# A hybrid recurrence and expert layer: the mixer in five token groups instead of four, and gathered rows paced closer

## The chip, the cores and the metric

One core of a Trainium2 chip runs the whole layer in one launch. The metric is the device time of one execution in microseconds; the runs before have a median of 3271.78 us. TensorE multiplies, VectorE and ScalarE and GpSimd work elementwise, SyncE issues the ordinary transfers and GpSimd the indirect ones (the gathers).

## What is computed

1024 tokens of width 1024 go through one layer and a last norm:

```
h   = rmsnorm(x);  proj = h @ w_in          # q, f, i, output gate, conv B C h, two merge gates
y_a = gated linear recurrence (8 heads x 64, chunks of 64 tokens, a 64x64 state per head)
y_b = B * causal_conv3(C * h)
x   = x + (sig(g_A) * (y_a @ w_hg) + sig(g_B) * (y_b @ w_conv)) @ w_out
h2  = rmsnorm(x)
# 8 heads: scores against two key sets of 128, top 16 of each, top 16 of the sums -> 128 experts
x   = x + sum over the picks of gate * gelu(u_e . h2) * v_e
out = rmsnorm(x)
```

The recurrence and the convolution carry a state from token to token, so groups of tokens run in order.

## The kernel before

**Two stages.** The mixer (all up to the picks) runs over groups of 256 tokens. The experts run in two ways: for tiles (128 tokens) 2 to 5 densely, over all 16384 experts, in a stage after the mixer (`dense`, line 1008); for tiles 0, 1, 6 and 7 by gathering the 128 picked rows of `peer_u` and then of `peer_v` (`gather`, line 890). One gathered row is an indirect transfer of 128x1024 f32 (0.524 MB) that GpSimd issues and one VectorE pass, line 930 for u, line 936 for v: 4 tiles x 128 x 2 = 1024 rows. Below, "row" means this.

**A group in the mixer.** `front` (line 486) transposes the normed tokens and does the convolution branch; `gates_b` and `gates_a` multiply the merge gates; `recurrence` runs four pairs of heads one behind the other (`decays`, then `chunks`); `post` (line 598) does w_hg, w_out (line 624), the second norm, the query matmuls and the key scores (line 657) with their top 16; `picks_of` makes the expert numbers of each tile (`idx`, line 864). The helper `whole` (line 245) holds nearly all weight matmuls: the weights of 128x128 stand, the group's tokens move, so a matmul has as many columns as the group has tokens. Each group fetches all weights again, in blocks that `block` (line 239) puts into a ring of six buffers of 4 KB per partition (`wraw`). In the trace an f32 matmul is two records.

**What sets the order.** `together` (line 381) runs these generators side by side: it always advances the one whose share of its expected TensorE time (T_REC, T_POST and so on) is least, so it sets the order of the work by a clock of its own. Rows come in through `paced` (line 367): as soon as tile 0 has its `idx`, a step of four rows (two u, two v, once both run), then a pause of ROW_STEP on that clock. In the mixer rows have four buffers of 4 KB (line 329), in the dense stage four more (line 363). In the dense stage `interleave` (line 410) spreads the steps that are left, of ROW_STEPS = 290, evenly over the stage's TensorE time. `all_gates` (line 955) makes the gate table of the dense tiles by one-hot products (line 997 on VectorE, line 974 on TensorE) beside the last two groups, from group FROM on. A scheduler then fixes each engine's order; each engine runs it in order.

Of the kernel before, what the change touches and what calls it, by code (L numbers as in the profile page):

```python
# [22 lines left out]
P = 128  # L23
D = 1024
KK = D // P
TOKENS = 1024
GROUP = 256
CHUNK = 64
HALF = CHUNK // 2
# [27 lines left out]
RUSH = 5.4  # L57
ROWS_AT_ONCE = 4
T_REC, T_GATES, T_W, T_POST, T_FRONT, T_PICK = 92.0, 6.4, 55.0, 92.0, 170.0, 10.89
T_SOON, T_ROWS, ROW_STEP = 300.0, 1e4, 7.5  # L60
FROM = 2
T_GB, T_FIRST = 27, 40.0
ROW_STEPS, T_DENSE = 290, 1330.0

# [59 lines left out]
class Layer:  # L124
# [198 lines left out]
    def schedule(self):  # L323

        nd, last = len(DENSE) * P, self.place_dense()
        self.wd = self.dram.tile([nd // TB, P, NKEYS, TB], F32, tag="wd", name="wd")
        self.wraw = self.ring(0, 4, 6)
        self.M = M = self.place()
        self.rows = self.ring(300, 4, 4)
        rows = self.gather(BY_ROW)  # L330
        with contextlib.ExitStack() as parts:
            for name in ("w", "h0", "h1", "yy", "y", "o"):
                parts.enter_context(self.fresh(name))
            parts.enter_context(self.fresh("a", side="right"))
            self.gmix, self.gffn = self.view(M.gmix_kb, [D]), self.view(M.gffn_kb, [D])
            self.nc.sync.dma_start(self.gmix, self.a["norm_mix_g"].broadcast_to([P, D]))
            G = [types.SimpleNamespace(no=g, n0=GROUP * g, q=g % 2, ready=False, conv=False) for g in range(TOKENS // GROUP)]
            run_all(self.front(G[0], self.first_norm(G[0])))
            self.nc.sync.dma_start(self.gffn, self.a["norm_ffn_g"].broadcast_to([P, D]))
            for g in G:  # L340
                must = [(self.recurrence(g), T_REC), (self.gates_b(g), T_GB), (self.gates_a(g), T_GATES)]
                more = []
                if g.no:
                    must.append((self.post(G[g.no - 1]), T_SOON if g.no == 1 else T_POST))
                    more.append((self.picks_of(G[g.no - 1]), T_PICK))
                if g.no + 1 < len(G):
                    nxt = G[g.no + 1]
                    more.append((self.front(nxt, list(self.first_norm(nxt))), T_FRONT if g.no else T_FIRST))
                if g.no == 1:
                    more.append((self.paced(rows), T_ROWS))  # L350
                if g.no == FROM:
                    M.lev = self.ring(48, 8)
                    more.append((self.all_gates(DENSE, G[3]), T_W))
                self.together(must, more)
            self.together([(self.post(G[3]), T_POST)], [], True)
        self.regions = ALWAYS | EXPERTS
        with contextlib.ExitStack() as parts:
            for name in ("v", "raw", "s1", "s0", "ht", "e0"):
                parts.enter_context(self.fresh(name))
            for name in ("e1", "ph"):  # L360
                parts.enter_context(self.fresh(name, side="right"))
            self.whi, self.wlo, self.wraw = last.whi, last.wlo, last.wraw
            self.rows.more(last.rows)
            self.interleave(zipped(self.dense(last, DENSE[0] * P, nd), self.picks_of(G[3]), 4), rows)
            run_all(rows)

    def paced(self, rows):
# [108 lines left out]
    def first_norm(self, G):  # L476

        nc, a, M = self.nc, self.a, self.M
        xs = [M.xs.take([D]) for _ in range(2)]
        for t, x in enumerate(xs):  # L480
            nc.sync.dma_start(x, a["x"][G.n0 + t * P:G.n0 + (t + 1) * P, :])
        for x, r in zip(xs, self.rstd(xs)):
            nc.vector.scalar_tensor_tensor(x, x, r, self.gmix, op0=ALU.mult, op1=ALU.mult)
            yield x

    def front(self, G, xs):

        nc, M, n = self.nc, self.M, GROUP
        G.ready = G.conv = False
        while G.no > 1 and self.posted < G.no - 2:  # L490
            yield 1
        G.h = h = self.view(M.h[G.q], [KK, n])
        G.y = y = self.view(M.y, [4, n])
        for t, x in enumerate(xs):
            self.transpose_whole(h, x, t)
            yield
        G.ready = True
        while self.mixed < G.no - 1:
            yield 1
        for j in range(4):  # L500
            cc = self.whole(self.w_in(BCC + j), h, KK, n)
            ccs = M.f0.take([n])
            nc.scalar.copy(ccs, cc[:, :n])
            ch = self.whole(self.w_in(BCH + j), h, KK, n)
            u = M.fu.take([n + 2])
            nc.vector.tensor_copy(u[:, 0:2], self.carry[:, j, :])
            nc.vector.tensor_tensor(u[:, 2:], ccs, ch[:, :n], op=ALU.mult)
            nc.vector.tensor_copy(self.carry[:, j, :], u[:, n:n + 2])
            yield
            cb = self.whole(self.w_in(BCB + j), h, KK, n)  # L510
            s = M.f1.take([n])
            nc.scalar.activation(s, u[:, 0:n], AF.Copy, scale=self.convw[:, j, 0:1])
            for i in (1, 2):
                nc.vector.scalar_tensor_tensor(s, u[:, i:i + n], self.convw[:, j, i:i + 1], s,
                                               op0=ALU.mult, op1=ALU.add)
            nc.vector.tensor_tensor(y[:, j, :], s, cb[:, :n], op=ALU.mult)
            yield
        G.conv = True
# [3 lines left out]

    def gates_b(self, G):

        nc, M, n = self.nc, self.M, GROUP
        while self.picked < G.no - 2 or not G.conv:
            yield 1
        G.mb = self.view(M.big[G.q], [KK, n])
# [8 lines left out]

    def gates_a(self, G):

        nc, n = self.nc, GROUP  # L540
        while self.picked < G.no - 2:
            yield 1
        G.sga = self.view(self.M.big[G.q] + 8, [KK, n])
        for c in range(8):
            gp = self.whole(self.w_in(BGA + c), G.h, KK, n)
            nc.scalar.activation(G.sga[:, c, :], gp[:, :n], AF.Sigmoid)
            yield

    def recurrence(self, G):

        nc, M, n, w = self.nc, self.M, GROUP, self.w_in
        while not G.ready:
            yield 1
        h = G.h
# [42 lines left out]

    def post(self, G):

        nc, a, M, n = self.nc, self.a, self.M, GROUP  # L600
        nt, n0 = n // P, G.n0
        mg = self.view(M.h[G.q], [KK, n])
        for c in range(8):
# [47 lines left out]
        def scores(c, qt):  # L651
# [6 lines left out]
            s = M.s.take([n])  # L658
            nc.scalar.copy(s, sp[:, :n])
            todo.extend((top[:, t, c, :], topi[:, t, c, :], s[:, t * P:(t + 1) * P]) for t in range(nt))  # L660
            if len(todo) == 8:
                self.top16(todo)
                todo.clear()

# [12 lines left out]
    def picks_of(self, G):  # L677

        while self.posted < G.no:
            yield 1  # L680
        for t in range(GROUP // P):
            yield from self.pick(G.n0 // P + t, G.top[:, t], G.topi[:, t], G.mem)
        self.picked = G.no

    def decays(self, qs, k, b):
# [1 line left out]

        nc, m = self.nc, GROUP  # L690
        lv = self.M.lev.take([8, m])
        for li, ln in enumerate(LEVELS):
            b0, b1 = halves(b, ln)
# [21 lines left out]

    def chunks(self, p, lv, el, qs, k, v, hgs, y):

        nc, M, m = self.nc, self.M, GROUP
        ops = [self.ps(), self.ps()]
        for t in range(m // P):  # L720
            gps = []
# [457 lines left out]
```

## Time and profile before

| | |
|---|---|
| device time, three runs | 3261.70, 3271.78, 3284.35 us (median 3271.78) |
| the profiled execution | 3261.81 us, span 3260.0 us |
| TensorE busy | 2805.7 us, 86% |
| VectorE busy | 2646.3 us, 81% |
| GpSimd busy | 1537.4 us, 47% |
| ScalarE busy | 1002.6 us, 31% |
| moved | 938 MB, 288 GB/s over the span |

The page gives busy times of engines as shares of the whole span; since the mixer and the dense stage have different limits, the rows below are cut by stage. "Idle before" and "waited for" name what ended an engine's wait.

### The profile page before, as it was taken

The numbers are of one execution on the slowest core, as the hardware profiler recorded it, in microseconds if no ns is written. First come the engines' busy times: TensorE is split into PE (matmuls) and PEld (weight loads), VectorE is DVE, ScalarE is ACT, GpSimd is POOL, SyncE is SP. The second block draws the span as 40 slices with busy tenths as digits, with TensorE's granted clock in tenths as the row PEclk, the third lists the DMA queues.
The fourth block names the chain that finished last, engine by engine and source line by source line (L and its number), as shares of the span: only waits on it lengthen the run. The fifth ranks groups of instructions, "written<-read, shape, count | busy, mean of one in ns | idle before, by whom it ended". The sixth has DMA issues, their size and how long they took to land.

```text
span 3260.0 us, 42632 instructions
## 1 busy us (share of the span) xinstructions
PE 2805.7 (86%) x14956; PEld 2380.9 (73%) x14956; DVE 2646.3 (81%) x5515; ACT 1002.6 (31%) x1537; POOL 1537.4 (47%) x1332
## 2 busy tenths in 40 slices
PE   8998999898986989944649999999999999999910
PEld 7887888687775878734537778888888888888800
DVE  2233378578899898998999999889989888898897
ACT  3223133413314553113333333333333333333200
POOL 0001025355554445565355665546555555465575
PEclk9998999798997989967859999999999999999955
DMA  6442548498884888978888899989999999999998
GB/s 200 142 127 91 171 137 278 159 350 280 289 320 130 325 326 307 318 253 305 280 287 306 287 369 362 351 306 359 367 338 343 343 349 344 308 370 347 331 356 297
DMA packets 321718, 937.98 MB, mean 288 GB/s; under 512 B 29280, under 2 KB 103520, under 8 KB 319456
## 3 DMA queue, kind: packets, MB, share of 16 engines
q0 software_dynamic: 147456, 536.94, 46.2%
q1 hardware_dynamic: 174048, 398.32, 35.0%
q8 instruction: 118, 1.93, 0.2%
q14 instruction: 96, 0.79, 0.1%
HBM read 889.01 MB, written 46.14 MB: 287 GB/s over the span
## 4 chain that ended last, share of the span: by engine, by line
PE 59%; DVE 23%; DMA 6%; issue 6%; POOL 3%; ACT 2%; SPq 0%; DVEq 0%; POOLq 0%; ACTq 0%
PE ps L1053 14%; PE ps L249 14%; PE ps L285 13%; PE ps L288 6%; DVE mem_g L936 5%; DVE mem_g L930 4%; DMA mem_g<-in_peer_u,idx 3%; DMA mem_g<-in_peer_v,idx 2%; PE ps L624 2%; PE ps L731 2%; PE ps L278 2%; PE ps L277 2%; PE ps L276 2%; DVE mem_y L997 1%; POOL mem_g L900 1%
## 5 line engine op out<-in xcount | busy, mean ns | idle before, releaser
L249 PE MATMUL ps<-mem_h,mem_w 128*128 128x256 f32 x3584 | 836.2, 391 | 2.9 <-DVE mem_z L534 2.9
L249 PEld LDWEIGHTS ps<-mem_h,mem_w 128*128 128x128 f32 x3584 | 692.9, 196 | 102.4 <-DVE mem_z L534 3.2
L900 POOL DMA_INDIRECT mem_g<-in_peer_u,idx x352 | 441.3, 1254 | 455.7 <-DVE mem_g L930 283.0
L900 POOL DMA_INDIRECT mem_g<-in_peer_v,idx x336 | 404.8, 1205 | 377.5 <-DVE mem_g L936 236.1
L1053 PE MATMUL ps<-mem_v,mem_ph 128*128 128x512 f32 x2304 | 552.2, 389 | 3.3 <-DVE mem_ph L237 2.6
L285 PE MATMUL ps<-mem_ht,mem_s 128*128 128x512 f32 x2048 | 508.5, 390 | 5.9 <-DVE mem_z L1064 5.9
L1053 PEld LDWEIGHTS ps<-mem_v,mem_ph 128*128 128x128 f32 x2304 | 432.0, 188 | 95.3 <-DVE mem_ph L237 4.9
L930 DVE SCALAR_TENSOR_TENSOR mem_g<-mem_g 128x1024 f32<-128x1024 f32 x352 | 444.9, 1270 | 41.6 <-DMA mem_g<-in_peer_u,idx 41.0
L936 DVE SCALAR_TENSOR_TENSOR mem_g<-mem_g 128x1024 f32<-128x1024 f32 x336 | 444.9, 1324 | 35.0 <-DMA mem_g<-in_peer_v,idx 33.8
L285 PEld LDWEIGHTS ps<-mem_ht,mem_s 128*128 128x128 f32 x2048 | 385.2, 188 | 87.8 <-DVE mem_z L1064 7.6
L236 ACT ACTIVATE mem_s<-mem_raw 128x512 fp32r<-128x512 f32 x256 | 161.3, 632 | 578.4 <-PE ps L285 550.6
L900 POOL DMA_INDIRECT mem_e<-in_peer_v,idx x176 | 224.9, 1278 | 195.2 <-DVE mem_g L936 153.7
L288 PE MATMUL ps<-mem_ht,mem_s 128*128 128x512 f32 x1024 | 273.7, 389 | 0.0
L900 POOL DMA_INDIRECT mem_e<-in_peer_u,idx x160 | 205.0, 1281 | 136.1 <-DVE mem_e L930 89.0
L696 POOL TENSOR_TENSOR mem_y<-mem_y 128x128 f32<-128x128 f32 x96 | 53.2, 554 | 413.7 <-DVE mem_y L565 413.6
L936 DVE SCALAR_TENSOR_TENSOR mem_g<-mem_e,mem_g 128x1024 f32<-128x1024 f32 x176 | 226.5, 1287 | 13.3 <-DMA mem_e<-in_peer_v,idx 7.7
L237 DVE TENSOR_TENSOR mem_s<-mem_raw,mem_s 128x512 fp32r<-128x512 f32 x256 | 180.0, 707 | 64.0 <-PE ps L288 50.3
L288 PEld LDWEIGHTS ps<-mem_ht,mem_s 128*128 128x128 f32 x1024 | 192.4, 188 | 40.0
L930 DVE SCALAR_TENSOR_TENSOR mem_e<-mem_e,mem_g 128x1024 f32<-128x1024 f32 x160 | 196.8, 1236 | 2.9 <-DMA mem_e<-in_peer_u,idx 2.9
L236 ACT ACTIVATE mem_v<-mem_z 128x1024 fp32r<-128x1024 f32 x128 | 129.5, 1053 | 185.5 <-PE ps L278 182.8
L857 POOL TENSOR_TENSOR mem_z<-mem_z 128x800 f32<-128x800 f16 x64 | 124.9, 1951 | 101.3 <-DVE mem_z L855 58.0
L978 ACT COPY mem_a<-ps 128x512 f32<-128x512 f32 x128 | 124.2, 1084 | 130.5 <-PE ps L974 79.5
(189 smaller groups left out, 3841.4 us busy)
## 6 DMA issues: line engine op xcount, KB each, us to landing
mem_w<-in_w_in SPq DMA_DIRECT2D x160, 512.0 KB, 4.8
mem_raw<-in_peer_ut SPq DMA_DIRECT2D x128, 512.0 KB, 7.1
mem_z<-in_peer_v SPq DMA_DIRECT2D x128, 512.0 KB, 6.7
mem_w<-in_w_query SPq DMA_DIRECT2D x64, 512.0 KB, 4.9
wd<-mem_a SPq DMA_DIRECT2D x16, 2048.0 KB, 9.9
mem_z<-wd SPq DMA_DIRECT2D x32, 1024.0 KB, 14.1
mem_w<-in_w_out SPq DMA_DIRECT2D x32, 512.0 KB, 7.9
mem_w<-in_w_conv SPq DMA_DIRECT2D x32, 256.0 KB, 3.4
```

What stands on the lines that cost most here:

```text
L236: self.nc.scalar.activation(hi, src, AF.Copy)
L237: self.nc.vector.tensor_tensor(lo, src, hi.bitcast(F32), op=ALU.subtract)
L249: self.nc.tensor.matmul(ps, w[:, kk, :], act[:, kk, :], start=kk == 0, stop=kk == k - 1)
L276: mm(ps, lh, rh, start=first, stop=False, **kw)
L285: mm(ps, w[kk][0], act[part][:, kk, :], start=kk == part == 0, stop=False)
L288: mm(ps, w[j][1], act[0][:, j, :], start=False, stop=j == k - 1)
L857: nc.gpsimd.tensor_tensor(pr, eq, ci[:, hd:hd + 1, :].broadcast_to([P, TOPK, NCAND]), op=ALU.mult)
L900: nc.gpsimd.indirect_dma_start(out=r, out_offset=None, in_=a[table], in_offset=bass.IndirectOffsetOnAxis(ap=self.idx[t][:, k:k + 1], axis=0))
L930: nc.vector.scalar_tensor_tensor(u, u, 1.0, h2, op0=ALU.mult, op1=ALU.mult, accum_out=wt[:, k:k + 1])
L936: nc.vector.scalar_tensor_tensor(acc, v, wt[:, k:k + 1], acc, op0=ALU.mult, op1=ALU.add)
L978: nc.scalar.copy(dst[:, :, 4 * h:4 * h + 4].rearrange("p a t -> p t a"), ps.rearrange("p (t a) -> p t a", t=4))
L1053: nc.tensor.matmul(acc[t][hf], pp[c][i][:, tk], vp[c][:, k, 512 * hf:512 * hf + 512], start=c == 0 and i == 0 and k == 0, stop=c == NKEYS ...
```

## The change

The groups become 128, 128, 256, 256 and 256 tokens. Group sizes, tile counts and expected times (`share`) follow from the group. ROW_STEP falls from 7.5 to 6.2. FROM goes from 2 to 3, which is the same tokens (512 to 767) as before, and the two big buffers alternate so that the last group has the one it had. The diff, cut to its core:

```
+GROUPS = (128, 128, 256, 256, 256)
-T_SOON, T_ROWS, ROW_STEP = 300.0, 1e4, 7.5
-FROM = 2
+T_SOON, T_ROWS, ROW_STEP = 300.0, 1e4, 6.2
+FROM = 3
...
-            G = [types.SimpleNamespace(no=g, n0=GROUP * g, q=g % 2, ready=False, conv=False) for g in range(TOKENS // GROUP)]
+            G = [types.SimpleNamespace(no=g, n=n, n0=sum(GROUPS[:g]), q=(len(GROUPS) + g) % 2, share=n / GROUP,
+                                       ready=False, conv=False) for g, n in enumerate(GROUPS)]
+            end = G[-1]
...
-                must = [(self.recurrence(g), T_REC), (self.gates_b(g), T_GB), (self.gates_a(g), T_GATES)]
+                must = [(self.recurrence(g), T_REC * g.share), (self.gates_b(g), T_GB * g.share),
+                        (self.gates_a(g), T_GATES * g.share)]
...
-                    must.append((self.post(G[g.no - 1]), T_SOON if g.no == 1 else T_POST))
-                    more.append((self.picks_of(G[g.no - 1]), T_PICK))
+                    old = G[g.no - 1]
+                    must.append((self.post(old), (T_SOON if g.no == 1 else T_POST) * old.share))
+                    more.append((self.picks_of(old), T_PICK * old.share))
...
-        xs = [M.xs.take([D]) for _ in range(2)]
+        xs = [M.xs.take([D]) for _ in range(G.n // P)]
...
-        nc, M, n = self.nc, self.M, GROUP
+        nc, M, n = self.nc, self.M, G.n
```

The last pair stands in `front`, `gates_b`, `gates_a`, `recurrence`, `post`, and alike in `decays`, `chunks` and `picks_of`.

Three places in the engines' order. TensorE, from the program's first matmul on; before (mem_h_153 is the transposed group, mem_w a weight block, mem_yy the convolution's result):

```order
L258 MATMUL ps<-c_ident,mem_a 128x128 x16
L249 MATMUL ps<-mem_h_153,mem_w 128x256 x112
L249 MATMUL ps<-mem_yy,mem_w 128x256 x4
L249 MATMUL ps<-mem_h_153,mem_w 128x256 x8
L258 MATMUL ps<-c_ident,mem_a 128x128 x8
```

and TensorE from the first matmul on in the changed kernel, whose lines are numbered a little higher:

```order
L259 MATMUL ps<-c_ident,mem_a 128x128 x8
L250 MATMUL ps<-mem_h_157,mem_w 128x128 x112
L250 MATMUL ps<-mem_yy,mem_w 128x128 x4
L250 MATMUL ps<-mem_h_157,mem_w 128x128 x8
L259 MATMUL ps<-c_ident,mem_a 128x128 x8
```

The sequence and the count of weight matmuls stay, each has half the columns, and half the transposes stand ahead.

VectorE where the first tile's expert numbers are made (`idx`), before; the first row (line 930) stands 29 lines of this list further on:

```order
L831 TENSOR_TENSOR mem_z<-mem_z 128x8x8
L767 SCALAR_TENSOR_TENSOR st_117<-st_118,el,ps 64x64 x2
L864 CAST idx<-mem_z 128x128
L818 CAST mem_z<-mem_z 128x256
L802 MAX mem_z<-mem_z 128x8 x8
L820 TENSOR_SCALAR mem_z<-mem_z 128x8x16
L804 MATCH_REPLACE rest<-mem_z 128x50
```

and VectorE at the first `idx` in the changed kernel (line 935 is the u row's pass, 512 to 521 the convolution of a following group):

```order
L863 TENSOR_REDUCE mem_z<-mem_z 128x16
L869 CAST idx<-mem_z 128x128
L521 TENSOR_TENSOR mem_yy<-mem_a,ps 128x256
L935 SCALAR_TENSOR_TENSOR mem_g<-mem_g 128x1024 x2
L512 TENSOR_TENSOR mem_a<-mem_a,ps 128x256
L935 SCALAR_TENSOR_TENSOR mem_g<-mem_g 128x1024
L513 COPY carry<-mem_a 128x2
L519 SCALAR_TENSOR_TENSOR mem_a<-mem_a,c_convw 128x256 x2
```

Rows follow at once, since the pick of a second tile of the same group no longer stands behind the first.

VectorE at the program's end, behind the dense tiles' last norm passes (line 951), before; these rows are the end of a longer run, 66 rows in all:

```order
L936 SCALAR_TENSOR_TENSOR mem_g<-mem_e_10537,mem_g 128x1024 x2
L936 SCALAR_TENSOR_TENSOR mem_g<-mem_e_10541,mem_g 128x1024 x2
L936 SCALAR_TENSOR_TENSOR mem_g<-mem_g 128x1024 x4
L936 SCALAR_TENSOR_TENSOR mem_g<-mem_e_10537,mem_g 128x1024 x2
L936 SCALAR_TENSOR_TENSOR mem_g<-mem_e_10541,mem_g 128x1024 x2
L936 SCALAR_TENSOR_TENSOR mem_g<-mem_g 128x1024 x4
```

and VectorE behind the same passes (line 956) in the changed kernel, the whole run up to the last tile's norm:

```order
L956 SCALAR_TENSOR_TENSOR mem_z<-mem_z,rstd,mem_raw 128x1024
L956 SCALAR_TENSOR_TENSOR mem_raw<-mem_raw,rstd 128x1024
L941 SCALAR_TENSOR_TENSOR mem_g<-mem_e_11853,mem_g 128x1024 x2
L941 SCALAR_TENSOR_TENSOR mem_g<-mem_e_11857,mem_g 128x1024 x2
L941 SCALAR_TENSOR_TENSOR mem_g<-mem_g 128x1024 x4
L941 SCALAR_TENSOR_TENSOR mem_g<-mem_e_11853,mem_g 128x1024 x2
```

66 rows behind the last dense norm became 10; the others stand earlier.

## Rows read from the trace of the kernel before

**Rows 1.** Windows by stage: bounds us, length, busy us by engine, clock, DMA share, GB/s.

```profile
0.00:452.00 452.00, 424.62 (x2519) 372.22 (x2519) 159.82 (x666) 138.18 (x237) 36.69 (x90) 0.97 0.46 145
452.00:681.50 229.50, 214.18 (x1243) 183.37 (x1242) 168.21 (x485) 68.64 (x111) 111.76 (x111) 0.90 0.65 221
681.50:1004.00 322.50, 274.05 (x1682) 236.19 (x1682) 273.96 (x834) 86.51 (x154) 166.81 (x156) 0.91 0.83 293
1004.00:1700.00 696.00, 494.84 (x3371) 435.26 (x3370) 632.72 (x1553) 254.68 (x370) 349.77 (x294) 0.83 0.81 286
1700.00:3107.00 1407.00, 1397.76 (x6146) 1153.87 (x6144) 1279.22 (x1796) 449.79 (x656) 775.59 (x595) 1.00 0.95 340
3107.00:3260.00 153.00, 0.21 (x1) 0.00 (x0) 132.36 (x186) 4.83 (x9) 96.75 (x89) 0.51 0.89 331
```

**Rows 2.** Timeline: start us, length, engine, line; VectorE at 492, TensorE at 680.

```profile
492.50 0.23 DVE L864 CAST idx<-mem_z 128x128 uint32<-128x128 f32 x1
...
679.80 1.89 PE L249 MATMUL ps<-mem_yy,mem_w 128*128 128x256 f32 x8
681.53 2.75 PE L624 MATMUL ps<-mem_w,mem_h 128*128 128x256 f32 x12
```

**Rows 3.** Groups by line and shape: VectorE's row passes, GpSimd's gather issues.

```profile
L930 DVE SCALAR_TENSOR_TENSOR mem_g<-mem_g 128x1024 f32<-128x1024 f32 x352 | 444.9, 1270 | 41.6 <-DMA mem_g<-in_peer_u,idx 41.0
L936 DVE SCALAR_TENSOR_TENSOR mem_g<-mem_g 128x1024 f32<-128x1024 f32 x336 | 444.9, 1324 | 35.0 <-DMA mem_g<-in_peer_v,idx 33.8
L936 DVE SCALAR_TENSOR_TENSOR mem_g<-mem_e,mem_g 128x1024 f32<-128x1024 f32 x176 | 226.5, 1287 | 13.3 <-DMA mem_e<-in_peer_v,idx 7.7 <-DMA mem_g<-x2d 4.3
L930 DVE SCALAR_TENSOR_TENSOR mem_e<-mem_e,mem_g 128x1024 f32<-128x1024 f32 x160 | 196.8, 1236 | 2.9 <-DMA mem_e<-in_peer_u,idx 2.9
...
L900 POOL DMA_INDIRECT mem_g<-in_peer_u,idx x352 | 441.3, 1254 | 455.7 <-DVE mem_g L930 283.0 <-issue 33.5 <-DVE mem_z L810 32.4
```

**Rows 4.** Windows of line 930, then of line 936, alone: VectorE in the tail.

```profile
3107.00:3260.00 153.00, 29.26 (x48) 0.51 0.89 331
...
3107.00:3260.00 153.00, 91.09 (x71) 0.51 0.89 331
```

**Rows 5.** Timeline, VectorE at the end: the last rows and the last norm pass.

```profile
3249.07 2.60 DVE L936 SCALAR_TENSOR_TENSOR mem_g<-mem_e,mem_g 128x1024 f32<-128x1024 f32 x2
...
3255.08 1.28 DVE L951 SCALAR_TENSOR_TENSOR mem_g<-mem_g,rstd,mem_e 128x1024 f32<-128x1024 f32 x1
```

**Rows 6.** TensorE's waits: us, times, longest; 490 to 1004, then 1004 to 1690.

```profile
PE ps L876 <- DVE mem_z L872: 27.6, 1, 27.6
...
PE ps L974 <- DVE mem_y L997: 74.2, 15, 16.6
```

**Rows 7.** Timeline of TensorE at 366 us; the group of line 657's weight loads.

```profile
366.31 0.61 PE L657 MATMUL ps<-mem_z 128*128 128x128 f32 x4
366.75 2.97 PE L249 MATMUL ps<-mem_h,mem_w 128*128 128x256 f32 x13
...
L657 PEld LDWEIGHTS ps<-mem_z 128*128 128x128 f32 x256 | 38.8, 196 | 17.6 <-ACT mem_z L669 6.8 <-issue 5.5 <-ACT mem_a L978 1.9
```

**Rows 8.** Windows of line 249 alone: TensorE, its weight loads, clock, DMA.

```profile
0.00:452.00 452.00, 311.16 (x1387) 263.72 (x1387) 0.97 0.46 145
```

**Rows 9.** Transfers: GB/s in 40 slices; issues, KB each, median us to landing.

```profile
GB/s 200 142 127 91 171 137 278 159 350 280 289 320 130 325 326 307 318 253 305 280 287 306 287 369 362 351 306 359 367 338 343 343 349 344 308 370 347 331 356 297
...
mem_w<-in_w_in SPq DMA_DIRECT2D x160, 512.0 KB, 4.8
...
mem_e<-in_peer_v,idx POOLq DMA_INDIRECT x176, 7.5
```

**Rows 10.** VectorE's waits from 490 to 1004 us: us, times, longest.

```profile
DVE mem_g L930 <- DMA mem_g<-in_peer_u,idx: 23.2, 17, 4.1
DVE mem_g L936 <- DMA mem_g<-in_peer_v,idx: 15.0, 13, 3.1
```

**Rows 11.** Transfers from 490 to 1004 us: the v rows' issues, median us to landing.

```profile
mem_g<-in_peer_v,idx POOLq DMA_INDIRECT x62, 7.0
```

More of the change, by code (lines that the diff above doesn't have):

```diff
@@ L340, in schedule @@
             for g in G:
-                must = [(self.recurrence(g), T_REC), (self.gates_b(g), T_GB), (self.gates_a(g), T_GATES)]
+                must = [(self.recurrence(g), T_REC * g.share), (self.gates_b(g), T_GB * g.share),
+                        (self.gates_a(g), T_GATES * g.share)]
                 more = []
                 if g.no:
-                    must.append((self.post(G[g.no - 1]), T_SOON if g.no == 1 else T_POST))
-                    more.append((self.picks_of(G[g.no - 1]), T_PICK))
+                    old = G[g.no - 1]
+                    must.append((self.post(old), (T_SOON if g.no == 1 else T_POST) * old.share))
+                    more.append((self.picks_of(old), T_PICK * old.share))
                 if g.no + 1 < len(G):
                     nxt = G[g.no + 1]
-                    more.append((self.front(nxt, list(self.first_norm(nxt))), T_FRONT if g.no else T_FIRST))
+                    more.append((self.front(nxt, list(self.first_norm(nxt))), (T_FRONT if g.no else T_FIRST) * nxt.share))
                 if g.no == 1:
@@ L352, in schedule @@
                     M.lev = self.ring(48, 8)
-                    more.append((self.all_gates(DENSE, G[3]), T_W))
+                    more.append((self.all_gates(DENSE, end), T_W))
                 self.together(must, more)
-            self.together([(self.post(G[3]), T_POST)], [], True)
+            self.together([(self.post(end), T_POST)], [], True)
         self.regions = ALWAYS | EXPERTS
@@ L363, in schedule @@
             self.rows.more(last.rows)
-            self.interleave(zipped(self.dense(last, DENSE[0] * P, nd), self.picks_of(G[3]), 4), rows)
+            self.interleave(zipped(self.dense(last, DENSE[0] * P, nd), self.picks_of(end), 4), rows)
             run_all(rows)
@@ L523, in gates_b @@
     def gates_b(self, G):
-        nc, M, n = self.nc, self.M, GROUP
+        nc, M, n = self.nc, self.M, G.n
         while self.picked < G.no - 2 or not G.conv:
@@ L538, in gates_a @@
     def gates_a(self, G):
-        nc, n = self.nc, GROUP
+        nc, n = self.nc, G.n
         while self.picked < G.no - 2:
@@ L549, in recurrence @@
     def recurrence(self, G):
-        nc, M, n, w = self.nc, self.M, GROUP, self.w_in
+        nc, M, n, w = self.nc, self.M, G.n, self.w_in
         while not G.ready:
@@ L598, in post @@
     def post(self, G):
-        nc, a, M, n = self.nc, self.a, self.M, GROUP
+        nc, a, M, n = self.nc, self.a, self.M, G.n
         nt, n0 = n // P, G.n0
@@ L660, in scores @@
             todo.extend((top[:, t, c, :], topi[:, t, c, :], s[:, t * P:(t + 1) * P]) for t in range(nt))
-            if len(todo) == 8:
+            if len(todo) == 4 * nt:
                 self.top16(todo)
@@ L680, in picks_of @@
             yield 1
-        for t in range(GROUP // P):
+        for t in range(G.n // P):
             yield from self.pick(G.n0 // P + t, G.top[:, t], G.topi[:, t], G.mem)
@@ L685, in decays @@
     def decays(self, qs, k, b):
-        nc, m = self.nc, GROUP
+        nc, m = self.nc, b.shape[-1]
         lv = self.M.lev.take([8, m])
@@ L716, in chunks @@
     def chunks(self, p, lv, el, qs, k, v, hgs, y):
-        nc, M, m = self.nc, self.M, GROUP
+        nc, M, m = self.nc, self.M, qs.shape[-1]
         ops = [self.ps(), self.ps()]
```

## The prediction

> **What bounds the kernel now.** I read the profile by stages first, then by what each stage waits for. The windows table [rows 1] cuts the span at five places. Up to 452 us the mixer runs on the first tokens alone: TensorE is busy 424.6 of 452 us, VectorE 159.8. From 452 to 681.5 us (where the second group's w_out matmuls begin [rows 2]) TensorE still has 214 of 229.5 us. From 681.5 to 1004 us both are loaded (274 and 274 of 322.5), and from 1004 to 1700 us VectorE is the full one (633 of 696 against 495). From 1700 us, where the dense stage starts, TensorE has 1397.8 of 1407 us: the dense stage is TensorE-bound and takes 6144 matmuls of 128x512 that follow each other at 0.227 us. After 3107 us TensorE is done, and for 153 us only gathered rows remain.
>
> The second thing to see is where these rows lie. A row is one VectorE pass over 128x1024 (lines 930 and 936), 1024 of them, 1.28 us each: 444.9 + 444.9 + 226.5 + 196.8 = 1313 us over 1024 [rows 3]. Counted by stage (line 930 leaves two records for each, line 936 one; the tail's rows are shown [rows 4], the other stages read alike): 44 by 681.5 us, 108 more by 1004, 194 more by 1700, 583 in the dense stage, 95 in the tail. The first could not start before the first tile's expert numbers were there, at 492.5 us [rows 2].
>
> So the tail is late row work. 153 us for 95 rows is 1.61 us each; at 0.524 MB a row and 331 GB/s [rows 1] the transfer alone is 1.58 us. Row work taken out of the tail is gained there one for one, and paid wherever it is put instead.
>
> **The change, part by part.** The row counts below are counted in the order of VectorE's instructions of both kernels; times come from rows of the trace.
>
> *Where the rows go.* Before the first dense Gelu product (line 1028) stand 348 rows in the old order and 473 in the new; between it and the last one 572 and 525; behind the last one 104 and 26. So 125 rows enter the mixer, 47 leave the dense stage and 78 leave the end.
>
> *Tail.* The last TensorE work stands where it stood. Behind it the new order has the sums of line 1112 (4 us), the small operations of two norms (about 8) and their two last passes (2.5), 12 rows at 1.58 us (19), two more norm passes (2.5), 10 rows (8 are fetched ahead, so by the VectorE price: 13), and then the same end as now: 3249.07 + 2.6 is the last row, 3260 the end [rows 5], 8.3 us. Together about 57 instead of 153: **-96 us**. Bounds -85 (all 22 rows at 1.58 and the norms in line) and -104 (rows all landed).
>
> *Dense stage.* TensorE's instructions are the same; VectorE has 47 rows fewer and was already not the bound (1279 of 1407). **0 us**, bounds -5 and +5.
>
> *Middle: from the w_out matmuls of tokens 256 to 511 to the dense stage.* TensorE's work is the same in both orders, instruction for instruction. VectorE's order has 316 rows here before and 343 after: 27 more, 34.6 us. In the part until all_gates starts (681.5 to 1004 us, VectorE 85% busy) there are 8 of them, which can lie under TensorE's work; the other 19 (24 us) fall where VectorE is 91% busy and TensorE waits for its one-hot products (74.2 us for line 997 [rows 6]). **+27 us**, bounds 0 and +45.
>
> *Head: to those same w_out matmuls, now 681.5 us.* Three sub-steps.
>
> First, the matmuls. 512 of the 2048 weight matmuls (line 249) belong to the first 256 tokens; they become 1024 with 128 columns. A matmul is two records. With 256 columns they start 0.216 us apart (8 in 1.73 us, from 679.80 to 681.53 [rows 2]); the trace has no weight matmul of 128 columns, but the key scores of line 657 are the same f32 shape with their own weight loads, and four of them start within 0.44 us (366.31 to 366.75), 0.11 each [rows 7]. So a half-size matmul costs 0.222 instead of 0.432 us, and the 1024 cost 227 us instead of 221: +6 us. The bound on the other side: a load lasts 196 ns [rows 7], and if it did not lie beside the matmul before it, nothing would be saved by halving the columns; that is a rival below. The Trainium skill's page "TensorE: Matmul & The Clock Gate" (Part 3, "The mechanism") says a weight load overlaps with matmuls in flight only where their row groups differ; these use all rows, so by it each half-size matmul would pay its loads openly. The records of line 657 don't bear that out: they start 0.11 us apart with their loads beside them. By the rule the sum would be some 215 us longer.
>
> Second, when rows may start. TensorE's 424.6 us up to 452 are 311.2 of line 249 [rows 8] and 113 of the rest; the first group of 128 tokens has as many line 249 records up to its last key scores (680 matmuls in either order) at half the price, 156 us, and half the rest, 57. With the 27 us of idle kept, that is 239 us; the pick chain to the expert numbers took 40 us (452 to 492.5) and works on one tile either way. So the first tile's numbers come at about 280 us, not 492.5.
>
> Third, what happens from 280 us to those w_out matmuls. TensorE's busy time in the head is 424.6 + 214.2 = 639 us now [rows 1] and 645 in the new kernel; 213 of it and some 37 in the pick chain's 40 us are done by 280, so 395 are left. VectorE's order has 130 rows ahead of that group's first product of line 606, against 32 now: 98 more, 126 us, on an engine that has 328 us of work in 681.5 [rows 1]. The stage where rows already run at 0.33 a us is 681.5 to 1004: without the one 27.6 us stall at line 876 [rows 6] TensorE is busy 274 of 295 us there, 93%. 395 at 93% is 425, so w_out comes at 705 us, +24 us. Transfers speak against so little. Weights are fetched once per group (160 blocks of w_in for four groups [rows 9]), and a fifth group fetches all of them again: 40 blocks of w_in, 16 of w_query, 8 of w_out and 4 of w_v at 512 KB, 16 of w_hg and w_conv at 256 KB and 1 MB of keys, 41 MB. Up to 681.5 us the old kernel moved 65.5 + 50.7 = 116 MB [rows 1]; the new one moves 41 MB of weights and 51 MB of rows more, 208 MB. By 280 us it has moved about 67: 680 matmuls at 65.5 KB, 56 of lines 588 and 624 at 131 KB, 6 MB of tokens, keys and prefetch, 9 MB in the pick chain's time. 141 MB in 425 us would be 332 GB/s. The mixer's slices reach 350 at most, and the stages with rows 286 to 293 on average [rows 1, 9]. At 310 GB/s, about halfway, it takes 455 us, with w_out at 735. I take that: **+53 us**, bounds +24 (TensorE alone) and +80 (293 GB/s: 481 us).
>
> Cover: a weight block of 512 KB lasts TensorE 3.46 us now and 1.78 us with 128 columns; six blocks are fetched ahead, so 10.7 us cover a landing of 4.8 us [rows 9]. When transfers are full and landings double, the cover is gone, and the loss is that of the 293 GB/s case. The extra 1.3 us table loads and issues of SP for a fifth group lie on engines that are far from full (ScalarE 138 of 452 [rows 1]).
>
> **Sum.** +53 + 27 + 0 - 96 = -16. The profiled execution took 3261.8 us by the clock outside (span 3260.0), the median of the three runs is 3271.8, 0.3% above it. 3261.8 - 16 = 3246, times 1.003 is 3256; I say **3255 us**.
>
> **The rivals.**
>
> *The mixer swallows the rows.* For it: VectorE idles 292 us before 452 us [rows 1], and rows made it wait for their transfer only 38 us in all from 490 to 1004 us [rows 10]. Against it: the 332 GB/s. Head +24, middle 0: -72, so 3190, or 3199 beside the median.
>
> *Transfers bound the head.* The first two groups' weights and the rows get no more than the stage mean of 293 GB/s: head +80, middle +27, net +11, 3283 beside the median. For it: the DMA share is 0.83 from 681.5 us on already. Against: slices at 350.
>
> *Rows come late, on the other side.* All rows in the mixer use four buffers. One turn of a buffer is the landing (7.0 us for the v rows [rows 11]), the issue on GpSimd (1.25 [rows 3]) and the multiply (1.28): four in 9.5 us, 0.42 rows a us; the middle needs 343 in about 1046, 0.33. VectorE runs in order, so a late row holds the recurrence's operations behind it, and TensorE behind those. At landings of 11.7 us the pace is 0.28 a us: 343 rows take 1221 us, +202; net +53 + 202 - 96 = +159, about 3431. It makes the kernel slower by 1% from head and middle together +129 on, which is a landing of 10.4 us. Against it: the rows that land in the busier second half take 7.5 us in the median, with twice the buffers [rows 9].
>
> *Weight loads bind.* For it: a load's 196 ns [rows 7] is more than 0.11, and if loads can't lie beside matmuls, the half-size ones cost 0.432 instead of 0.222: 1024 x 0.21 = +215 us, net +199, 3471. Against it: the starts of line 657. It is the case that the rule of the Trainium skill's page named above would give.
>
> **How the numbers follow.** Forecast 0.56 (its own range 3220 to 3280), swallowed 0.17, transfers 0.15, rows late 0.08, loads 0.04. A measurement of this kernel can tell about 1% from no change, that is below 3239 or above 3304. Below: the swallowed case and 0.20 of the forecast, 0.37. Above: the two slow cases and 0.03 of the transfer case, 0.15. Within: 0.48. The range reaches down to the swallowed case's edge and up past the transfer case, and leaves out the two slow ones: 3190 to 3310.
>
> **What would show it.** In the changed profile: the first idx at about 280 us (right if 260 to 310); 128-column records of line 249 about 0.11 us apart while nothing is waited for; the w_out matmuls of tokens 256 to 511 at about 735 us; the dense stage's first matmul at about 1780 us; 1407 us of dense stage; a tail of about 57 us. I am wrong if the first idx is not there by 350 us, if the slices between 280 and 735 us show TensorE waiting for weights, if row landings rise over 10 us, or if the dense stage gets longer than 1412 us.

## The result, and the profile after

The changed kernel takes 3245.16 us (median of 6 runs, 3238.13 to 3252.48) beside 3267.47 for the kernel before on the same chip: a ratio of 0.9927, 95% interval 0.9900 to 0.9955. That is 0.7% faster: less than the 1% that the prediction took for the least a measurement can tell, but clear of the noise, since the interval lies below 1. It is ten us below the 3255 that were forecast. The profiled execution took 3238.13 us (span 3236.4).

Windows by stage of the changed kernel, cut at the same events as [rows 1] (first `idx`, w_out of tokens 256 to 511, start of `all_gates`, dense stage, TensorE's end); columns as there:

```profile
0.00:301.00 301.00, 263.18 (x2271) 252.27 (x2272) 135.55 (x607) 126.57 (x240) 38.60 (x98) 0.94 0.71 240
301.00:743.40 442.40, 394.83 (x2523) 349.49 (x2522) 332.84 (x846) 149.34 (x255) 228.43 (x256) 0.92 0.85 305
743.40:1077.00 333.60, 275.16 (x1682) 238.72 (x1682) 291.69 (x848) 86.85 (x154) 172.28 (x170) 0.90 0.86 303
1077.00:1783.60 706.60, 498.25 (x3372) 436.31 (x3371) 654.97 (x1579) 259.18 (x373) 385.76 (x307) 0.83 0.82 292
1783.60:3190.30 1406.70, 1399.20 (x6145) 1157.19 (x6144) 1221.88 (x1713) 449.68 (x657) 736.10 (x549) 0.99 0.90 323
3190.30:3236.40 46.10, 0.19 (x1) 0.00 (x0) 40.18 (x85) 3.99 (x8) 15.95 (x14) 0.53 0.62 228
```

Against [rows 1]: the head is 62 us longer (743.4 for 681.5), the middle 22 (1040.2 for 1018.5), the dense stage the same, the tail 107 shorter (46.1 for 153); the sum is -24. TensorE's busy time in the head rose by 19 (263.18 + 394.83 against 638.80), so 43 of the 62 are idle time. The rise is in the weight matmuls, here in a window of the whole head, line 249 before and line 250 after (the first numbers are TensorE's busy time and its records):

```profile
0.00:681.50 681.50, 478.58 (x2096) 404.46 (x2096) 0.94 0.53 170
...
0.00:743.40 743.40, 499.44 (x3120) 458.35 (x3120) 0.93 0.79 278
```

The timeline answers to [rows 2, 7]: weight matmuls of 128 columns, the first expert numbers, and the w_out matmuls (line 629 now):

```profile
19.77 20.49 PE L250 MATMUL ps<-mem_h,mem_w 128*128 128x128 f32 x182
...
301.20 0.23 DVE L869 CAST idx<-mem_z 128x128 uint32<-128x128 f32 x1
...
743.45 1.89 PE L629 MATMUL ps<-mem_w,mem_h 128*128 128x256 f32 x8
```

182 half-size records in 20.49 us are 0.113 us each, with nothing waited for. The v rows of the tail, in a window of line 941 alone (its first numbers are the window's length and VectorE's busy time), answer to [rows 4]; 22 rows are left of 95:

```profile
3190.30:3236.40 46.10, 28.18 (x22) 0.53 0.62 228
```

What TensorE waited for longest in the head (us, times, longest), before, from 0 to 681.5 us:

```profile
PE ps L258 <- DVE mem_a L483: 15.9, 1, 15.9
PE ps L731 <- DVE mem_y L711: 11.2, 2, 7.1
PE ps L756 <- DVE st L767: 4.0, 6, 0.7
```

and in the changed kernel, from 0 to 743.4 us:

```profile
PE ps L761 <- DVE st L772: 21.7, 6, 12.7
PE ps L736 <- DVE mem_y L715: 17.1, 3, 8.6
PE ps L259 <- DVE mem_a L488: 14.5, 1, 14.5
PE ps L662 <- DMA mem_z<-in_keys: 11.4, 5, 3.8
PE ps L250 <- ACT mem_h L260: 7.4, 1, 7.4
```

Line 761 (756 before) is the recurrence's matmul with the state that line 772 makes; 736 (731) follows the decays of 715; 259 (258) are the program's first transposes. Line 662 waits for the transfer of a block of the key set, line 250 once for ScalarE's copy of the transposed tokens. No wait of a weight matmul is for a weight block.

A second profile of the same kernel shows how far such stages can be trusted. In it the head takes 754.1, the middle 1055.9, the dense stage 1405.9 and the tail 46.8. Its execution was the slowest of its 6 runs (span 3262.7; their median 3247.63), while that of the first profile was the fastest of its 6. Head and middle move by 11 and 16 us between them; dense stage and tail do not.

### The profile page after: what moved, and what is told of

Read it like the earlier page. It is cut to its first block, busy times and chain, and to the rows that moved or that the text cites. A ratio compares the mean times of both kernels' runs of the same rounds, so it can differ in the third digit from the quotient of the medians.

```text
span 3236.4 us, 45285 instructions
## 1 busy us (share of the span) xinstructions
PE 2830.8 (87%) x15988; PEld 2434.0 (75%) x15988; DVE 2677.1 (83%) x5673; ACT 1075.6 (33%) x1686; POOL 1577.1 (49%) x1392
## 4 chain that ended last, share of the span: by engine, by line
PE 56%; DVE 23%; DMA 9%; issue 5%; ACT 3%; POOL 3%; SPq 0%; DVEq 0%; POOLq 0%; ACTq 0%
PE ps L1058 15%; PE ps L286 14%; PE ps L250 10%; PE ps L289 7%; DVE mem_g L941 5%; DMA mem_g<-in_peer_u,idx 4%; DVE mem_g L935 4%; DMA mem_g<-in_peer_v,idx 4%; PE ps L277 2%; PE ps L278 2%; PE ps L279 2%; PE ps L736 1%; DMA mem_z<-in_keys 1%; DVE mem_z L863 1%; DVE mem_y L1002 1%
## 5 line engine op out<-in xcount | busy, mean ns | idle before, releaser
L250 PE MATMUL ps<-mem_h,mem_w 128*128 128x256 f32 (+1 forms) x4480 | 856.8, 350 | 10.4 <-ACT mem_h L260 8.7
L250 PEld LDWEIGHTS ps<-mem_h,mem_w 128*128 128x128 f32 x4480 | 743.4, 200 | 88.0 <-ACT mem_h L260 10.2
L905 POOL DMA_INDIRECT mem_g<-in_peer_u,idx x384 | 486.6, 1267 | 503.6 <-DVE mem_g L935 305.1
L905 POOL DMA_INDIRECT mem_g<-in_peer_v,idx x368 | 450.8, 1225 | 442.2 <-DVE mem_g L941 202.2
L941 DVE SCALAR_TENSOR_TENSOR mem_g<-mem_g 128x1024 f32<-128x1024 f32 x368 | 494.9, 1345 | 50.3 <-DMA mem_g<-in_peer_v,idx 50.0
L935 DVE SCALAR_TENSOR_TENSOR mem_g<-mem_g 128x1024 f32<-128x1024 f32 x384 | 487.1, 1272 | 38.4 <-DMA mem_g<-in_peer_u,idx 37.6
L905 POOL DMA_INDIRECT mem_e<-in_peer_u,idx x128 | 186.4, 1456 | 220.9 <-DVE mem_e L935 192.4
L905 POOL DMA_INDIRECT mem_e<-in_peer_v,idx x144 | 173.3, 1203 | 139.9 <-DVE mem_g L941 94.0
L941 DVE SCALAR_TENSOR_TENSOR mem_g<-mem_e,mem_g 128x1024 f32<-128x1024 f32 x144 | 184.3, 1280 | 1.3 <-DMA mem_g<-x2d 1.1
L701 POOL TENSOR_TENSOR mem_y<-mem_y 128x128 f32<-128x128 f32 (+1 forms) x120 | 60.1, 501 | 233.4 <-DVE mem_y L570 233.3
L935 DVE SCALAR_TENSOR_TENSOR mem_e<-mem_e,mem_g 128x1024 f32<-128x1024 f32 x128 | 156.7, 1230 | 1.5 <-DMA mem_e<-in_peer_u,idx 1.5
```

The source lines that it names most:

```text
L250: self.nc.tensor.matmul(ps, w[:, kk, :], act[:, kk, :], start=kk == 0, stop=kk == k - 1)
L905: nc.gpsimd.indirect_dma_start(out=r, out_offset=None, in_=a[table], in_offset=bass.IndirectOffsetOnAxis(ap=self.idx[t][:, k:k + 1], axis=0))
L935: nc.vector.scalar_tensor_tensor(u, u, 1.0, h2, op0=ALU.mult, op1=ALU.mult, accum_out=wt[:, k:k + 1])
L941: nc.vector.scalar_tensor_tensor(acc, v, wt[:, k:k + 1], acc, op0=ALU.mult, op1=ALU.add)
```

## The experiments

Lines of the changed kernel stand five above those of the kernel before: rows are lines 935 (u) and 941 (v), the transposes of a second norm 259, that norm's products 643, the pick's matmuls 881. "Head" is the time to the w_out matmuls of tokens 256 to 511, "middle" from there to the dense stage.

**The two halves alone.** First the groups without the shorter distance, then the distance without the groups.

```
-T_SOON, T_ROWS, ROW_STEP = 300.0, 1e4, 6.2
+T_SOON, T_ROWS, ROW_STEP = 300.0, 1e4, 7.5
```

> The new groups with the old ROW_STEP of 7.5. VectorE's order then has 440 rows ahead of the dense stage (473 in the changed kernel, 348 before), 567 in it (525, 572) and 17 behind its last Gelu product (26, 104). My theory (a row costs its 1.28 us of VectorE in the mixer, nothing in the dense stage, 1.6 us in the tail): 33 rows fewer in the mixer are worth 30 to 42 us, the dense stage stays at 1407 us, the tail at 35 to 45 us, so about 3195 to 3210 us beside 3245 for the changed kernel: the closer pace is then no part of the gain but a loss. Rival (the closer pace brings the gain, the groups cost): 3250 to 3270 us, no faster than the changed kernel.

3268.62 us, ratio 0.9987 (0.9972 to 1.0001): far above my theory's range, inside the rival's.

```
-T_SOON, T_ROWS, ROW_STEP = 300.0, 1e4, 7.5
+T_SOON, T_ROWS, ROW_STEP = 300.0, 1e4, 6.2
```

> The old four groups with ROW_STEP 6.2. The order has 390 rows ahead of the dense stage (348 before), 575 in it, 59 behind its last Gelu product (104). My theory: the tail loses 45 rows, -71 us; the mixer gets 42 more, between +27 (half of them hidden) and +54; together -44 to -17, about 3225 to 3250 us beside 3267 before. Rival (the mixer before 1000 us has room for rows only because the first numbers come earlier): the 42 rows cost more than their VectorE time, no gain, 3260 to 3280.

3276.14 us, ratio 1.0018 (1.0007 to 1.0030). Here too the time lies in the rival's range and not in my theory's. Neither half gains anything, though both shorten the tail (to 30 and 90 us from 153): their middles take 1073 and 1083 us, with 322 and 350 rows, and the changed kernel's with 343 rows takes 1040. So the middle does not go by the number of rows alone.

**Rows held back.** The changed kernel, its rows starting only when the second tile has its numbers:

```
-        while 0 not in self.idx:
+        while 1 not in self.idx:
```

> The changed kernel, with rows starting only when the second tile has its numbers: 16 rows stand ahead of the third group's first product of line 606 (130 in the changed kernel, 32 before), 348 ahead of the dense stage, 923 to its end, as before the change. So it is the price of the small groups alone. Theory 1 (the head's 62 us come from rows standing in VectorE's order between the recurrence's operations): w_out of tokens 256 to 511 at 690 to 705 us instead of 743, total 3275 to 3290. Theory 2 (the small groups themselves cost them, by short recurrences with nothing beside them): w_out at 725 to 743, total 3310 to 3330. Theory 3 (my prediction's, transfers): 157 MB by then at 310 GB/s after the first 67, w_out near 700, as theory 1; the next kernel tells these two apart.

3347.47 us, ratio 1.0231 (1.0214 to 1.0248). No theory's total holds, and the head lies between theory 1 and theory 2: it takes 714.2, the middle 1071 (TensorE stands 42.8 us at line 259 in it), the tail 150. Its windows of the head and of the tail:

```profile
0.00:301.00 301.00, 262.54 (x2260) 252.04 (x2261) 133.72 (x603) 126.03 (x240) 38.61 (x98) 0.94 0.71 238
301.00:714.20 413.20, 389.77 (x2535) 345.55 (x2534) 194.99 (x671) 143.84 (x250) 95.12 (x143) 0.95 0.56 185
...
3199.60:3349.50 149.90, 0.39 (x2) 0.00 (x0) 129.02 (x183) 4.97 (x11) 91.75 (x85) 0.52 0.88 328
```

So of the head's 62 us the small groups cost 33 with hardly any rows (24 in the head, 44 before the change; TensorE 13.5 busier, 19 more idle), at 185 GB/s, far from full transfers; the 115 rows more of the changed kernel cost 29, a quarter us each.

**A quarter of the weights.** The changed kernel, where the second group of 128 tokens fetches a quarter of each weight block; the rest of its weights is left out, the matmuls stay. The edit, cut to its core (`thin` is set while the second group's work is handed in):

```
+        part = dims[0] // 4 if self.thin else dims[0]
-        self.nc.sync.dma_start(raw, src)
+        self.nc.sync.dma_start(raw[:, :part], src[:, :part])
...
```

> The changed kernel, where the second group of 128 tokens fetches only a quarter of each weight block and uses what lies in the rest of the buffer: about 30 MB less in the head, TensorE, VectorE and rows as they are (140 rows instead of 130 ahead of the third group's line 606). It leaves out part of that group's weights. My prediction's theory (transfers bound the head): the 30 MB at 310 GB/s are worth most of 97 us of transfer time, so w_out of tokens 256 to 511 comes at 705 to 715 us instead of 743, total 3210 to 3220. Rival (waits for VectorE and ScalarE, and the half clock behind them): w_out stays within 8 us of 743, total 3238 to 3252.

3245.23 us, the time of the changed kernel. Its head:

```profile
0.00:301.00 301.00, 262.14 (x2283) 251.99 (x2284) 138.87 (x609) 126.39 (x240) 39.74 (x99) 0.95 0.59 194
301.00:759.40 458.40, 396.94 (x2510) 350.90 (x2510) 343.44 (x855) 152.54 (x257) 249.25 (x264) 0.90 0.78 270
```

With 270 instead of 305 GB/s the w_out matmuls come no sooner: 759.4, beside 743.4 and 754.1 in the changed kernel's two profiles (this execution, at 3252.19 us, was the slowest of its four). The 30 us that the transfers' theory asked for are not there. Transfers don't bound the head.

**What holds the middle of the halves.** TensorE's waits with the groups alone, 1160 to 1572 us:

```profile
PE ps L259 <- DVE mem_z L643: 55.0, 1, 55.0
PE ps L881 <- DVE mem_z L877: 32.2, 1, 32.2
```

ScalarE in that wait (start, length, line; in brackets idle time before it and what ended it). Line 947 is the Gelu of a block of gathered products, 230 the square of a norm, first tile 0's last norm (mem_g), then the group's second norm (mem_z):

```profile
1250.21 1.28 ACT L947 ACT_TABLE_LOAD   x1
1295.91 0.23 ACT L947 ACTIVATE mem_g<-mem_g 128x32 f32<-128x32 f32 x1 [44.42 <-DVE mem_g L935]
1299.21 1.06 ACT L230 ACTIVATE junk<-mem_g 128x1024 f32<-128x1024 f32 x1 [3.07 <-DVE mem_g L941]
...
1300.39 1.06 ACT L230 ACTIVATE junk<-mem_z 128x1024 f32<-128x1024 f32 x1
```

And VectorE, one row after the other, most of them waiting for their transfer:

```profile
1287.67 1.22 DVE L935 SCALAR_TENSOR_TENSOR mem_g<-mem_g 128x1024 f32<-128x1024 f32 x1 [1.29 <-DMA mem_g<-in_peer_u,idx]
...
1289.71 1.29 DVE L941 SCALAR_TENSOR_TENSOR mem_g<-mem_g 128x1024 f32<-128x1024 f32 x1 [0.81 <-DMA mem_g<-in_peer_v,idx]
1291.85 1.23 DVE L935 SCALAR_TENSOR_TENSOR mem_g<-mem_g 128x1024 f32<-128x1024 f32 x1 [0.85 <-DMA mem_g<-in_peer_u,idx]
```

The group's norm stands behind tile 0's last norm, and this behind the 288th row (tile 0's last v row). In the code both norms, and the sixteen largest of the pick, take one scratch buffer (`rest`, one copy), and the norms share four small vectors. Where tile 0's norm was handed in first, the others must wait for its rows; in VectorE's order 22 rows stand together just ahead of it. New theory A: this shared scratch, not the rows' number, spoils the halves. In the changed kernel row 288 is done in time; ScalarE there squares tile 0's norm 44 us ahead of the group's, and TensorE's wait at line 259 is 2.7 us:

```profile
1198.71 1.06 ACT L230 ACTIVATE junk<-mem_g 128x1024 f32<-128x1024 f32 x1 [0.58 <-DVE mem_g L941]
...
1242.77 1.06 ACT L230 ACTIVATE junk<-mem_z 128x1024 f32<-128x1024 f32 x1
```

The test gives tile 0's norm scratch of its own (a row buffer for the square, and likewise its own `ms`, `rstd`, `rs_y`, `rs_t`), in the groups alone; the edit, cut to its core:

```
-        r, = self.rstd([x])
+        r, = self.rstd([x], self.rows.take([D]), "_own")
...
-        junk = self.small.tile([P, D], F32, tag="rest", name="junk", bufs=1)
+        if junk is None:
+            junk = self.small.tile([P, D], F32, tag="rest", name="junk", bufs=1)
...
```

> The small groups with the old distance of 7.5 between row steps, as in the run with the groups alone (3268.6 us, where TensorE stood 55 us before the transposes of a norm, line 259), but the last norm of a gathered tile takes scratch of its own (the square's output in a row buffer, its four small vectors under names of their own) in place of the scratch that all norms share. In VectorE's order the 22 rows that stood together ahead of that norm are spread, and 431 rows instead of 440 stand ahead of the dense stage. Theory A (the shared scratch chains the norm of the third group behind the norm of tile 0, and so behind the 288th row; TensorE waits for that): the 55 us wait falls under 20, the stage from the w_out matmuls of tokens 256 to 511 to the dense stage falls from 1073 to about 1030, total 3220 to 3235. Theory B (the rows' count and their VectorE time make the middle long): 9 rows fewer, 12 us, total 3250 to 3262.

3227.34 us, ratio 0.9874 (0.9851 to 0.9897), 18 below the changed kernel. The middle takes 1015 us instead of 1073. Its windows with the groups alone, then with own scratch (length first, the third busy time is VectorE's):

```profile
752.40:1825.40 1073.00, 785.54 (x5054) 683.22 (x5052) 919.77 (x2397) 346.48 (x527) 518.02 (x461) 0.83 0.79 278
...
752.40:1767.50 1015.10, 774.52 (x5053) 673.66 (x5051) 905.41 (x2378) 340.87 (x524) 507.73 (x447) 0.85 0.81 287
```

VectorE is 14 us less busy (9 rows fewer) and 44 less idle.

ScalarE now squares the group's norm first, and tile 0's 85 us later:

```profile
1230.55 1.06 ACT L231 ACTIVATE junk<-mem_z 128x1024 f32<-128x1024 f32 x1
...
1234.71 1.05 ACT L231 ACTIVATE junk<-mem_z 128x1024 f32<-128x1024 f32 x1
...
1319.76 1.06 ACT L231 ACTIVATE mem_g<-mem_g 128x1024 f32<-128x1024 f32 x1 [4.35 <-DVE mem_g L942]
```

and the transposes (line 260 here) wait 1.6 us:

```profile
1250.11 1.97 PE L260 MATMUL ps<-c_ident,mem_z 128*128 128x128 f32 x8 [1.60 <-DVE mem_z L644]
```

**The same in the other half.** The distance alone, with that scratch:

> The kernel before with the distance of 6.2 between row steps, as in the run with the step alone (3276.1 us, where TensorE stood 84.6 us for the pick's product of line 872), and scratch of its own for the last norm of a gathered tile. 360 rows instead of 390 stand ahead of the dense stage, and 85 instead of 59 behind the last first-half product of that stage. Theory A (in the run with the step alone the pick's sixteen largest waited with the shared scratch for tile 0's norm and its 288th row): the longest wait of TensorE ahead of the dense stage falls from 84.6 to 50 or less, the stage from the w_out matmuls of tokens 256 to 511 to the dense stage falls from 1078 to 1025 to 1045, the tail grows from 90 to about 130, total 3255 to 3275. Theory B (the wait is the pick chain's own length plus its rows): the longest wait stays over 70, the stage falls by the 30 rows' 38 us at most, total 3275 to 3290.

3252.57 us, ratio 0.9955 (0.9943 to 0.9967). TensorE's wait for the pick, 1092 to 1700 us, with the distance alone (us, times, longest):

```profile
PE ps L876 <- DVE mem_z L872: 131.7, 2, 84.6
```

and with own scratch:

```profile
PE ps L877 <- DVE mem_z L873: 78.9, 2, 43.5
```

The middle falls from 1083 to 1011, more than theory A asked; the 30 rows that left it are part of that, 38 us at 1.28 each. The tail is 131, as expected, and the total a little below the range.

**Own scratch where nothing is late for it.** First in the kernel before, then in the changed kernel.

> The kernel before with scratch of its own for the last norm of a gathered tile and nothing else; 347 rows instead of 348 ahead of the dense stage, 104 behind its last first-half product in both. In VectorE's order the norm of the last group stood behind tile 0's norm, which waits for the 288th row, with three rows between the products it needs and that row. Theory A: those three or four rows, 5 to 10 us, are saved in the middle; total 3255 to 3268, so nearly the same as the kernel before: the shared scratch was no large cost until rows came earlier and closer. Theory E (own scratch helps by itself, and the good of the run with the small groups came from it and not from the earlier rows): 3225 or less.

3273.88 us, ratio 1.0024 (1.0013 to 1.0036): no gain, a little beyond the expected range.

> The changed kernel with the same scratch of its own for the last norm of a tile. Its order of VectorE hardly changes (474 rows instead of 473 ahead of the dense stage, no rows in a clump in either), because the 288th row was already done when the third group's norm came. Theory A (the shared scratch matters only where rows are late for it): same as the changed kernel, 3240 to 3250. Theory C (own scratch helps by itself, by more slack at every norm): 3225 or less.

3260.05 us, ratio 0.9960 (0.9943 to 0.9977): not the 3240 to 3250 expected. By the ratios it is some 10 us slower than the changed kernel (0.9927 and, below, 0.9933), but the intervals overlap. Head 750.2, middle 1051.6, dense stage 1410; the stages are those of the changed kernel's second profile. Whether own scratch costs anything here is open. Both runs say that it is no gain by itself.

**Rows that stand together, but not ahead of the norm.**

```
-T_SOON, T_ROWS, ROW_STEP = 300.0, 1e4, 6.2
+T_SOON, T_ROWS, ROW_STEP = 300.0, 1e4, 5.9
```

> The changed kernel with a distance of 5.9 between row steps in place of 6.2. 474 rows instead of 473 stand ahead of the dense stage, but 12 of them now stand together, up to the 288th, ahead of tile 0's last norm, and the products that the third group's norm needs (line 635) come behind that norm. Theory A (only the shared scratch makes rows cost TensorE there, and this norm is free of it in time): no wait over 25 us for line 259, total 3238 to 3255. Theory D (rows that stand together cost wherever they stand, some 2 us each, for they run at the pace of the transfers): about 25 us more, total 3262 to 3275.

3254.58 us, ratio 0.9956 (0.9939 to 0.9972), inside theory A's range, at its upper edge; the wait at line 259 is 2.7 us, as A says. The middle of 1054.6 is that of the other runs with as many rows.

**Faster handing out in the dense stage.**

```
-ROW_STEPS, T_DENSE = 290, 1330.0
+ROW_STEPS, T_DENSE = 290, 1290.0
```

> The changed kernel with the assumed TensorE time of the dense stage 1290 in place of 1330, which hands the rows out faster in that stage: 1008 rows stand ahead of the last first-half product of that stage instead of 998, and the last norms of two more tiles follow without rows between them. Theory (the tail is priced by its late rows, 1.6 us each, and the dense stage has VectorE time to spare): dense stage unchanged at 1407 us, tail 46 to about 34, total 3230 to 3238. Rival (VectorE near the end of the dense stage is already as full as it can be, so that rows put there hold TensorE): dense stage 1412 or more, total 3243 to 3255.

3239.01 us, ratio 0.9902 (0.9881 to 0.9923): tail 35.5 and dense stage 1406.0, about as expected. It is 6 below the changed kernel, which the intervals don't separate.

**The best and the changed kernel side by side.**

> The changed kernel once more, beside the next one on the same chip, to see how far two profiles of one kernel differ by stage. Total 3240 to 3250; the w_out matmuls of tokens 256 to 511 and the dense stage's first matmul within 10 us of the first profile's 743.4 and 1783.6. Were the first profile's stages a rare case, they would move by 20 or more.

> Small groups, the old distance of 7.5 and scratch of its own for a tile's last norm, once more. If it beats the changed kernel: 3220 to 3235, 10 to 25 us below the run beside it, and no wait of TensorE for line 260 over 20 us behind 1100 us. If the first result was chance: within 5 us of the run beside it.

3247.63 (ratio 0.9933, 0.9917 to 0.9950) and 3231.06 (0.9885, 0.9865 to 0.9904): the groups with the old distance and own scratch beat both kernels, the changed one by 17 us. That the changed kernel's second profile would lie within 10 us of its first was wrong (754.1 for 743.4, and the dense stage at 1810.0 for 1783.6): by the expectation's own sign, a move of 20 or more, the first profile's stages are not typical. Windows of the own-scratch kernel's middle, dense stage and tail:

```profile
753.90:1773.70 1019.80, 769.19 (x5054) 670.64 (x5052) 907.99 (x2381) 340.83 (x524) 506.70 (x448) 0.86 0.81 286
1773.70:3189.80 1416.10, 1400.59 (x6144) 1155.79 (x6144) 1281.40 (x1779) 449.86 (x654) 778.03 (x593) 0.99 0.95 337
3189.80:3229.30 39.50, 0.39 (x2) 0.00 (x0) 34.91 (x82) 5.64 (x10) 10.76 (x9) 0.55 0.63 229
```

## Why the prediction was right, and where it was not

The stages add up to -24 us for the -16 reckoned. The total is nearer than its parts: a head 9 too long is more than made up by a tail 11 and a middle 5 shorter than reckoned.

**First idx**: 301 for 280, inside its bound of 310. By then TensorE has been busy 263 us for the 250 reckoned, and idle 38 for 30.

**Half-size matmuls**: right where nothing is waited for, 0.113 us a record for the 0.111 taken from line 657's records, a load beside each. Over the whole head the weight matmuls cost 21 us more (499.4 for 478.6), not 6; with the rows held back 19 (497.4), so rows don't explain it, and why is open. The case that loads bind falls. With it falls here the word "only" in the rule that the Trainium skill's page "TensorE: Matmul & The Clock Gate" (Part 3, "The mechanism") gives on row groups: these loads use all rows and did not hold the matmuls up. The paragraph ahead of that rule also lets a load for the background weight buffer go ahead of matmuls in flight, which the prediction left out.

**Head, +53**: the size was near (+62, and +73 in the second profile), the reason wrong, so the nearness is luck. The step that failed is "At 310 GB/s". The transfers did run at about that pace (305 GB/s from 301 us on), but they don't set the time: with a quarter of a group's weights the head is as long, and with the rows held back it is 33 longer than before at 185 GB/s. The 62 are +19 of TensorE's busy time (the +6 of halved matmuls was too small) and +43 of waits. The waits for the recurrence's state grew by 18 us (21.7 for 4.0), those for its decays by 6, those for the keys' transfers from nothing to 11.4 (8.5 with the rows held back, at 185 GB/s, so not from full transfers), those for ScalarE's copy from nothing to 7.4. My reading, not tested by itself: small groups give TensorE less work to put between such steps (the 33 with hardly any rows), and rows ahead of the steps in VectorE's order lengthen them (the 29). The division by TensorE's 93% busy share was the step that left these waits out. That transfers bound the head is refuted as a rival too.

**Middle, +27**: right in size, and the mechanism holds where the shared scratch is free. With 313 to 320 rows (the kernel before, and own scratch in it, in the groups alone, twice, and in the distance alone) it takes 1011 to 1020, mean 1016. With 343 or 344 rows (the changed kernel twice, and with the 5.9 distance, the dense rate, own scratch) it takes 1040 to 1056, mean 1050. That is 34 us for 28 rows, 1.2 each; the prediction had 1.28 for 19 of 27. The run with a quarter of the weights has 332 rows there and takes 1035, on the line between. VectorE's idle time tells the same: 94 to 113 us of the middle in all these runs, but 153, 143 and 141 with the groups alone, the distance alone and the rows held back. What the prediction did not see is the chain through the scratch. At 1.2 us a row from 1016 at 316 rows, these three stand 50, 26 and 36 us too high. For the first two the runs with own scratch show that the chain is the cause; for the rows held back it is taken from the 42.8 us wait at the same line, and own scratch was not tried. The changed kernel escapes it only by both edits together: with the small groups tile 0's numbers come early enough, with the short distance its 288 rows are done before the third group's norm. The rival "rows come late" (0.08) was judged by landings, from 10.4 us on. They stayed at 6.3 to 6.5 us (medians, 743 to 1783 us); the question was what stands behind the row. On ScalarE nothing behind the Gelu of line 947 started in its 44 us; the Trainium skill's page "PSUM — Partial Sum Buffer" ("Engine vs sequencer instructions") calls the queues of ScalarE, VectorE and GpSimd strict FIFO (in at one end, out at the other, in order), and for ScalarE the trace agrees.

**Dense stage, 0**: right, 1406.7 and 1405.9. With about 570 rows in it the halves, the rows held back and the own-scratch kernels with as many rows take 1413 to 1423, which looks as if rows no longer hid fully under TensorE's work. But the kernel before, also with 572, takes 1407, and the changed kernel with own scratch 1410 with 524. So the rows' number alone doesn't set it, and the cause is open.

**Tail, -96**: -107, just past the bound of -104. Its 22 rows cost 28.18 us, 1.28 each, not 1.58 for twelve of them; VectorE waits for no transfer there. That is 4 of the 11 us. The other 7 are the sums and norms, 18 us instead of the 25 reckoned: the prediction added them up one behind the other, and in the trace small steps of the second pair's norm lie between rows.

**The swallowed case** (-72) fails by the head (+62 for its +24) and by the middle (+22 for its 0), and not by the transfers that were held against it.

## What to carry to other kernels

Before you move work earlier on a filled engine, look for scratch it shares with work that another engine waits for: a single buffer turns "later in the order" into "behind everything the first user waits for". When two edits fail alone and work together, look for one event that both must bring in time. And price a head of small groups by the waits between dependent small steps, which busy shares and GB/s don't show.

## What the runs showed that was not expected

Two profiles of the same kernel differ by 26 us, all before the dense stage. In equal windows TensorE did fewer instructions in more busy time, at a granted clock of 0.91 for 0.92; the second profile's row, to be set beside the second row at the top:

```profile
301.00:743.40 442.40, 398.27 (x2499) 351.71 (x2498) 323.46 (x841) 148.99 (x253) 223.86 (x249) 0.91 0.84 297
```

So differences of stages below some 15 us need several profiles, and small differences of whole kernels need many timed runs of each.
